# Query projection of a latent attention in 12 tiles instead of 16, with rope parts moved by DMA

## Chip, cores and metric

One core of a Trainium2 chip runs the whole program. The metric is the device time of one execution in microseconds (us), the median of several runs. The engines are TensorE (PE in the profile; its weight loads are PEld), VectorE (DVE), ScalarE (ACT), GpSimd (POOL) and SyncE (SP). SP starts the weight loads; ACT starts a few other transfers from its own queue.

## The reference, cut

Two layers of a decoder trunk on 512 positions of 1024 features, all in float32. The change lies in the latent attention of the first sub-layer: 16 heads, each with 64 features without rope and 32 with rope.

```python
def mla_attention(c_q, c_kv, k_rope, q_norm, w_uq, kv_norm, w_ukv, cos, sin):
    q = (rmsnorm(c_q, q_norm) @ w_uq).reshape(b, s, MLA_HEADS, QK_NOPE + QK_ROPE)
    q_nope = q[..., :QK_NOPE]
    q_pe = apply_rope(q[..., QK_NOPE:], cos[:, :, None, :], sin[:, :, None, :])
    kv = (rmsnorm(c_kv, kv_norm) @ w_ukv).reshape(b, s, MLA_HEADS, QK_NOPE + V_DIM)
    k_nope, v = kv[..., :QK_NOPE], kv[..., QK_NOPE:]
    k_pe = apply_rope(k_rope, cos, sin)          # one for all heads
    ...
        sc = (jnp.einsum('bqhd,bkhd->bhqk', q_nope[:, q0:kend], k_nope[:, :kend])
              + jnp.einsum('bqhr,bkr->bhqk', q_pe[:, q0:kend], k_pe[:, :kend]))
        ...
        pr = jax.nn.softmax(jnp.where(mask, sc, -jnp.inf), axis=-1).astype(v.dtype)
        outs.append(jnp.einsum('bhqk,bkhd->bqhd', pr, v[:, :kend]))
```

`apply_rope` gives t1*cos - t2*sin and t2*cos + t1*sin for the two halves of the 32 features. Around it in each layer stand the input projection, a state-space scan (`ssd`), the output projection, a cross-attention into 256 memory tokens and a gated MLP.

## The kernel before

Activations lie with features on the 128 partitions and the 512 positions along the free axis. Every float32 operand of a large product is split into a high part (float32r, written by ACT) and a low part (the rest, written by DVE or POOL), and `mm3` (L168 to L170) adds three products: high by high, high by low, low by high. Weights are fetched by SP into `wraw` (2 buffers) in the order of a hand-written plan (`specs`), then split by ACT (`whi`, L107) and mostly POOL (`wlo`, L108). All other tiles of 128x512 come from one tag, `unit()`, with `NU` = 68 buffers; PSUM is one tag of 8 banks, `bank()`. The order of TensorE is the order of the program text (`manual_schedule`); the other engines' orders are made by a list scheduler with the program order as priority.

Of the attention: `latent_q` projects the 384 query latents in three tiles and splits them. `front` computes the factors of the norms and the rotated key `kpe`, in generator steps that are interleaved with `inproj`, the projection of the scan's inputs. `prepare`, once, makes the tables `csa` (cos over signed sin, on partitions 64 to 127) and `csb` (the same on partitions 0 to 63), with ones in the other half. `key_tiles` puts the rotated key into the key tiles. `queries(h)` makes one tile of 128 rows for each head: 64 without rope, 32 with rope and the same 32 with their halves swapped. It needs nine matmuls of 128x512 (three `mm3`), one DVE product with the table (L661, it also carries the norm) and a split (L159 ACT, L162 DVE).

In `attention()` each head has one step, and its parts are issued in the order "SKVAMTQ": S scores and softmax of head h, K keys of the next pair (odd h), A product with the values for head h-2, M a tile of the memory keys, T transposes of the probabilities of head h-1, Q the query tile of head h+2. Queries 0 and 1 are made ahead, in `attention_head`. An odd step has K and, from step 3 on, M.

Softmax of one head is four chains: DVE mask and row maximum (L687), ACT exponential (L690), DVE reciprocal (L691), POOL scaling (L692). T is followed by splits (L159, L162) and a copy (L711), A by a copy (L732) and a sum (L733). In `front`, a small product (L455) needs `w`, the end of a chain of small DVE operations (L413 to L428).

## Time and profile before

| what | value |
|---|---|
| median of 3 runs | 1911.72 us (1911.09 to 1911.8) |
| the profiled execution | 1910.9 us |
| its span, first to last instruction | 1909.2 us |
| PE busy | 1871.1 us, 98% |
| DVE, ACT, POOL busy | 1030.6, 950.8, 886.3 us |

The profiled execution is 0.8 us below the median; 1.7 us of it lie outside the span. Busy time counts each engine's compute instructions; a transfer's issue is not in it, though it stands in the timeline on the queue of its engine (ACTq, SPq). Matmul records overlap: their pitch, not their length, is what each costs PE.

### The profile page before, as it was taken

How to read it: one execution, taken by the hardware profiler on the slowest of the kernel's cores; microseconds unless marked ns; L12 is line 12 of the kernel's file. 1: busy time of each engine (PE TensorE's matmuls, PEld its weight loads, DVE VectorE, ACT ScalarE, POOL GpSimd, SP SyncE). 2: the span in 40 equal slices, each digit the busy share in tenths (PEclk: the TensorE clock that was granted, in tenths of full speed). 3: DMA queues.
4: the chain of work that ended last, by engine and by line, in shares of the span. 5: the costliest groups of instructions: out<-in, count | busy, mean ns of one | idle time of the engine just before them, and what ended most of it. 6: DMA issues, size and time to landing. Idle time of an engine off the chain costs nothing.

```text
span 1909.2 us, 24928 instructions
## 1 busy us (share of the span) xinstructions
PE 1871.1 (98%) x9264; PEld 1574.3 (82%) x9264; DVE 1030.6 (54%) x1967; ACT 950.8 (50%) x1694; POOL 886.3 (46%) x563
## 2 busy tenths in 40 slices
PE   8899999999999999999999999999999999999998
PEld 6788889978888888888887887898788888888887
DVE  6777788843343555541137767887334445555312
ACT  5466588843345444433335557887333544444321
POOL 4436455555416444433354454555553354444232
PEclk9999999999999999999999999999999999999999
DMA  5233211332213233232222332113332122222322
GB/s 167 90 119 113 81 55 54 102 111 97 90 33 109 100 100 99 91 101 93 96 95 90 133 108 75 56 61 122 100 100 84 49 100 100 100 95 94 102 91 83
DMA packets 56025, 178.47 MB, mean 93 GB/s; under 512 B 6368, under 2 KB 9312, under 8 KB 55904
## 3 DMA queue, kind: packets, MB, share of 16 engines
q1 hardware_dynamic: 49984, 166.32, 26.4%
q10 hardware_dynamic: 5920, 10.55, 1.8%
q8 instruction: 73, 1.20, 0.3%
q14 instruction: 48, 0.39, 0.1%
HBM read 174.69 MB, written 2.16 MB: 93 GB/s over the span
## 4 chain that ended last, share of the span: by engine, by line
PE 91%; DVE 4%; ACT 2%; POOL 1%; issue 1%; DMA 1%; SPq 0%; ACTq 0%; POOLq 0%; DVEq 0%
PE ps L168 28%; PE ps L170 28%; PE ps L169 28%; PE ps L723 2%; PE ps L704 2%; ACT u L548 1%; POOL wlo L108 1%; DVE u L489 1%; ACT whi L107 1%; PE ps L584 1%; PE ps L578 0%; PE ps L924 0%; PE ps L726 0%; PE ps L558 0%; POOL rstd L271 0%
## 5 line engine op out<-in xcount | busy, mean ns | idle before, releaser
L108 POOL TENSOR_TENSOR wlo<-wraw,whi 128x1024 fp32r<-128x1024 f32 (+1 forms) x290 | 679.9, 2346 | 847.8 <-ACT whi L107 827.8
L168 PE MATMUL ps<-u,whi 128*128 128x512 f32 (+1 forms) x2326 | 899.7, 387 | 9.2 <-ACT whi L107 6.6
L169 PE MATMUL ps<-u,whi 128*128 128x512 f32 (+1 forms) x2326 | 890.6, 383 | 3.8 <-DVE u L165 3.8
L170 PE MATMUL ps<-u,wlo 128*128 128x512 f32 (+1 forms) x2326 | 890.7, 383 | 1.1 <-POOL wlo L108 0.6
L107 ACT ACTIVATE whi<-wraw 128x1024 fp32r<-128x1024 f32 (+2 forms) x319 | 328.2, 1030 | 505.6 <-PE ps L169 402.8
L168 PEld LDWEIGHTS ps<-u,whi 128*128 128x128 f32 x2326 | 439.3, 189 | 93.5 <-ACT whi L107 6.9
L170 PEld LDWEIGHTS ps<-u,wlo 128*128 128x128 f32 x2326 | 439.0, 189 | 87.6 <-POOL wlo L108 1.4
L169 PEld LDWEIGHTS ps<-u,whi 128*128 128x128 f32 x2326 | 439.5, 189 | 86.4 <-DVE u L165 4.9
L162 DVE TENSOR_TENSOR u<-ps,u 128x512 fp32r<-128x512 f32 (+2 forms) x236 | 136.8, 612 | 105.1 <-ACT u L159 104.2
L159 ACT ACTIVATE u<-ps 128x512 fp32r<-128x512 f32 (+2 forms) x236 | 117.3, 540 | 120.7 <-DVE ps L1013 98.3
L1009 DVE SCALAR_TENSOR_TENSOR u<-ps,small,u 128x510 f32<-128x510 f32 (+1 forms) x176 | 131.3, 749 | 74.9 <-ACT u L1007 72.0
L299 POOL TENSOR_TENSOR u<-u,u 128x512 f32<-128x512 f32 (+1 forms) x82 | 102.4, 1249 | 57.7 <-ACT u L298 56.4
L1002 DVE TENSOR_TENSOR ps<-ps,u 128x512 f32<-128x512 f32 x88 | 61.4, 700 | 109.7 <-PE ps L170 101.5
L108 DVE TENSOR_TENSOR wlo<-wraw,whi 128x1024 fp32r<-128x1024 f32 (+1 forms) x29 | 32.5, 1120 | 140.5 <-ACT whi L107 140.4
L692 POOL TENSOR_SCALAR u<-u,rs 128x512 f32<-128x512 f32 (+3 forms) x128 | 66.5, 533 | 78.4 <-DVE rs L691 74.3
L840 DVE TENSOR_TENSOR ps<-ps,u 128x512 f32<-128x512 f32 x32 | 22.4, 700 | 102.7 <-PE ps L170 102.7
L690 ACT ACTIVATE u<-ps,nm 128x512 f32<-128x512 f32 (+3 forms) x128 | 66.2, 524 | 18.0 <-DVE nm L687 12.0
L168 PE MATMUL ps<-u,u 128*128 128x512 f32 (+1 forms) x224 | 73.3, 327 | 0.9 <-ACT u L690 0.9
L489 DVE SCALAR_TENSOR_TENSOR u<-ps,half,u 128x511 f32<-128x511 f32 (+2 forms) x96 | 71.2, 744 | 3.0 <-ACT u L487 1.9
L170 PE MATMUL ps<-u,u 128*128 128x512 f32 (+1 forms) x224 | 72.1, 322 | 0.0
L169 PE MATMUL ps<-u,u 128*128 128x512 f32 (+1 forms) x224 | 72.0, 321 | 0.0
L1007 ACT ACTIVATE u<-ps,small 128x512 f32<-128x512 f32 x88 | 66.8, 761 | 1.7 <-DVE ps L1002 1.5
(193 smaller groups left out, 1765.6 us busy)
## 6 DMA issues: line engine op xcount, KB each, us to landing
wraw<-in_w_up SPq DMA_DIRECT2D x88, 512.0 KB, 3.4
wraw<-in_w_in SPq DMA_DIRECT2D x59, 512.0 KB, 3.5
wraw<-in_w_out SPq DMA_DIRECT2D x32, 512.0 KB, 3.4
wraw<-in_w_down SPq DMA_DIRECT2D x32, 512.0 KB, 3.4
u<-scr ACTq DMA_DIRECT2D x32, 256.0 KB, 4.0
wraw<-in_w_mk SPq DMA_DIRECT2D x16, 512.0 KB, 3.4
wraw<-in_w_mv SPq DMA_DIRECT2D x16, 512.0 KB, 3.5
wraw<-in_w_mq SPq DMA_DIRECT2D x16, 512.0 KB, 3.4
```

The source lines that it names most:

```text
L107: A.activation(hi[:, c], raw[:, c], AF.Copy)
L108: eng.tensor_tensor(lo[:, c], raw[:, c], hi[:, c].bitcast(F32), ALU.subtract)
L159: A.activation(hi, src, AF.Copy)
L162: (leng or V).tensor_tensor(lo, src, hi.bitcast(F32), ALU.subtract)
L168: T.matmul(o, lh, rh, start=start, stop=False)
L169: T.matmul(o, lh, rl, start=False, stop=False)
L170: T.matmul(o, ll, rh, start=False, stop=stop)
L299: (eng or G).tensor_tensor(self.acc, self.acc, sq, ALU.add)
L489: V.scalar_tensor_tensor(r_[:, d:], acc[:, :S - d], cw(3 - d), r_[:, d:], ALU.mult, ALU.add)
L692: G.tensor_scalar(p_[:, :n], p_[:, :n], rs[:, i:i + 1], 1.0, ALU.mult, ALU.mult)
L1007: A.activation(y, acc, AF.Identity, scale=fw(2), bias=par(layer, "ffn_b", ch))
L1009: V.scalar_tensor_tensor(y[:, d:], acc[:, :S - d], fw(2 - d), y[:, d:], ALU.mult, ALU.add)
```

## The change

`queries` now works on 12 tiles in the order `UQ`: a tile of -1 holds the rope parts of four heads (4 x 32 rows), any other the parts without rope of a pair of heads (2 x 64 rows). The swap of the halves and its sign move to the keys: the key tile now holds two rotated forms of the key, one that meets q*cos and one that meets q*sin. `query_rope` makes both products and splits each into one tile of `qph` and `qpl` (one buffer each); `query_pair` then moves, for each head of the pair, 32 rows of each of the four parts beside the head's 64 rows with DMAs that ACT issues. The norm moves from the tables to the latents (`cqr`), and `NU` goes from 68 to 64. The tiles are issued in steps 0, 1, 2, 4, 5, 6, 8, 9, 10 and 12 (`UQ_AT`), two ahead of the loop.

```diff
-NU = 68
+NU = 64
+UQ = (-1, 0, 1, -1, 2, 3, -1, 4, 5, -1, 6, 7)
...
+    UQ_AT = (0, 1, 2, 4, 5, 6, 8, 9, 10, 12)
...
-        for nm, i, n in (("w_uv", 0, 1024), ("w_uk", 0, 1024), ("w_uq", 0, 768)):
+        for nm, i, n in (("w_uv", 0, 1024), ("w_uq", 0, 768), ("w_uk", 0, 1024)):
...
-                elif part == "Q" and h % 2 == 0 and h + 2 < HEADS:
-                    plan("w_uq", layer, h // 2 + 1, 768)
+                elif part == "Q" and h in UQ_AT[::2]:
+                    plan("w_uq", layer, UQ_AT.index(h) // 2 + 1, 768)
...
     def prepare():
-        V.tensor_scalar(rnd, ang, 1.0 / (2 * math.pi), rc[:, 1:2], ALU.mult, ALU.add)
-        V.tensor_scalar(rnd, rnd, magic, None, ALU.add)
+        V.tensor_scalar(rnd, ang, 1.0 / (2 * math.pi), magic, ALU.mult, ALU.add)
...
-        phs = cp.tile([P, 1], F32, name="phs")
-        V.tensor_scalar(phs, rc[:, 1:2], 2 * math.pi, None, ALU.mult)
-        V.tensor_scalar(ang, ang, phs, None, ALU.add)
         V.tensor_scalar(ang, ang, 3.1415925, -3.1415925, ALU.min, ALU.max)
-        A.activation(tab, ang, AF.Sin)
-        V.tensor_scalar(tab, tab, rc[:, 2:3], None, ALU.mult)
-        G.memset(csa[0:64], 1.0)
-        V.tensor_copy(csa[64:128], tab[64:128])
-        V.tensor_copy(csb[0:64], tab[0:64])
-        G.memset(csb[64:128], 1.0)
+        A.activation(css, ang, AF.Sin)
+        A.activation(ang, ang, AF.Abs)
+        A.activation(csc, ang, AF.Sin, scale=-1.0, bias=quart)
...
-        csqa, csqb = unit(), unit()
         def latent_q(i):
             acc = proj(hid, "w_in", layer, i)
-            h_, l_ = unit(F32R), unit(F32R)
-            split(h_, l_, acc, par(layer, "q_norm", i))
+            r_ = unit()
+            A.copy(r_, acc)
             cqs.add(acc)
-            cqh.append(h_)
-            cql.append(l_)
+            cqr.append(r_)
...
         def front():
-            kro, ksh = unit(), unit()
-            V.tensor_tensor(kro[64:128], dtk[64:128], csa[64:128], ALU.mult)
-            A.copy(ksh[64:96], kro[96:128])
-            V.tensor_tensor(kpe[64:96], kro[64:96], ksh[64:96], ALU.add)
-            A.copy(kpe[0:32], kpe[64:96])
+            kro, krs, ksh = unit(), unit(), unit()
+            lo_, hi_ = slice(64, 96), slice(96, 128)
+            V.tensor_tensor(kro[lo_], dtk[lo_], csc[lo_], ALU.mult)
+            V.scalar_tensor_tensor(kro[hi_], dtk[hi_], rc[hi_, 1:2], css[hi_], ALU.mult, ALU.mult)
+            V.tensor_tensor(krs[lo_], dtk[lo_], css[lo_], ALU.mult)
+            V.scalar_tensor_tensor(krs[hi_], dtk[hi_], rc[hi_, 2:3], csc[hi_], ALU.mult, ALU.mult)
+            A.copy(ksh[lo_], kro[hi_])
+            A.copy(ksh[hi_], krs[lo_])
+            V.tensor_tensor(kpe[lo_], kro[lo_], ksh[lo_], ALU.add)
+            V.tensor_tensor(kpe[hi_], krs[hi_], ksh[hi_], ALU.add)
+            A.copy(kpe[0:64], kpe[64:128])
...
             pq = bcast(rq)
-            V.tensor_tensor(csqa, pq, csa, ALU.mult)
-            V.tensor_tensor(csqb, pq, csb, ALU.mult)
+            for i in range(3):
+                V.scalar_tensor_tensor(cqr[i], cqr[i], par(layer, "q_norm", i), pq, ALU.mult, ALU.mult)
+                h_, l_ = unit(F32R), unit(F32R)
+                split(h_, l_, cqr[i])
+                cqh.append(h_)
+                cql.append(l_)
...
         def key_tiles():
-                    for o in (0, 32):
-                        rr = slice(r0 + o, r0 + o + 32)
-                        A.copy(kh_[rr], kpe[r0:r0 + 32])
-                        V.tensor_tensor(kl_[rr], kpe[r0:r0 + 32], kh_[r0:r0 + 32].bitcast(F32), ALU.subtract)
+                    rr = slice(r0, r0 + 64)
+                    A.copy(kh_[rr], kpe[rr])
+                    V.tensor_tensor(kl_[rr], kpe[rr], kh_[rr].bitcast(F32), ALU.subtract)
...
-            V.tensor_tensor(acc, acc, csqb if h % 2 else csqa, ALU.mult)
-            qh, ql = unit(F32R), unit(F32R)
-            split(qh, ql, acc)
-            qq[h] = qh, ql
+        def query_rope(i):
+            acc, sn = query_tile(i), bank()
+            V.tensor_tensor(sn, acc, css, ALU.mult)
+            V.tensor_tensor(acc, acc, csc, ALU.mult)
+            ph, pl = new("qph", (P, 2, S), 1, F32R), new("qpl", (P, 2, S), 1, F32R)
+            for j, src in enumerate((acc, sn)):
+                split(ph[:, j], pl[:, j], src)
+            qpe[0] = ph, pl
+        def query_pair(i, pr):
+            acc = query_tile(i)
+            for j in range(2):
+                qh, ql = unit(F32R), unit(F32R)
+                rows, r0, s0 = slice(64 * j, 64 * j + 64), 64 - 64 * j, 32 * ((2 * pr + j) % 4)
+                for dst, src in zip((qh, ql), qpe[0]):
+                    for c in range(2):
+                        A.dma_start(dst[r0 + 32 * c:r0 + 32 * c + 32].bitcast(F32), src[s0:s0 + 32, c].bitcast(F32))
+                A.activation(qh[rows], acc[rows], AF.Copy)
+                V.tensor_tensor(ql[rows], acc[rows], qh[rows].bitcast(F32), ALU.subtract)
+                qq[2 * pr + j] = qh, ql
...
         def attention_head():
             yield from values(0)
+            query_rope(0)
+            yield
             keys(0)
-            queries(0)
-            yield
-            queries(1)
+            query_pair(1, 0)
             yield
```

`query_tile(i)` is the nine matmuls of `queries`, with a weight load at every even i. `ropec` and `w_uq` are laid out on the host to fit.

## Rows read from the trace of the kernel before

**Rows 1.** Page, part 1: busy us, share of span, instructions.

```profile
PE 1871.1 (98%) x9264; PEld 1574.3 (82%) x9264; DVE 1030.6 (54%) x1967; ACT 950.8 (50%) x1694; POOL 886.3 (46%) x563
```

**Rows 2.** Waits of PE, whole span: total us, times, longest.

```profile
PE ps L168 <- ACT whi L107: 6.6, 1, 6.6
PE ps L455 <- DVE dt L428: 6.5, 2, 4.3
...
PE ps L168 <- ACT u L690: 1.8, 4, 0.5
```

**Rows 3.** Busy time by stretch: PE, PEld, DVE, ACT, POOL, granted clock, DMA share, GB/s.

```profile
217.00:232.00 15.00, 13.13 (x82) 10.30 (x81) 12.53 (x24) 9.45 (x25) 4.23 (x2) 1.00 0.19 62
232.00:356.00 124.00, 122.56 (x765) 110.56 (x764) 101.85 (x302) 103.60 (x258) 73.38 (x80) 1.00 0.18 59
356.00:376.00 20.00, 20.00 (x129) 18.03 (x128) 15.32 (x41) 15.85 (x39) 8.85 (x12) 1.00 0.30 99
...
1173.00:1297.00 124.00, 122.56 (x767) 110.58 (x766) 102.07 (x301) 103.69 (x259) 73.61 (x80) 1.00 0.19 59
```

**Rows 4.** Timeline of PE, one query tile and the scores behind it.

```profile
322.05 0.47 PE L168 MATMUL ps<-u,whi 128*128 128x512 f32 x1
322.37 0.39 PE L169 MATMUL ps<-u,whi 128*128 128x512 f32 x1
...
323.98 0.39 PE L170 MATMUL ps<-u,wlo 128*128 128x512 f32 x1
324.21 0.39 PE L168 MATMUL ps<-u,u 128*128 128x512 f32 x1
```

**Rows 5.** Groups of ACT by shape, 232 to 356 us: busy, mean ns | idle before.

```profile
L159 ACT ACTIVATE u<-ps 128x512 fp32r<-128x512 f32 x27 | 16.1, 598 | 3.3 <-DVE ps L661 3.0
...
L647 ACT ACTIVATE u<-ps 64x512 fp32r<-64x512 f32 x14 | 8.2, 589 | 1.9 <-PE ps L170 1.7
...
L107 ACT ACTIVATE whi<-wraw 128x768 fp32r<-128x768 f32 x6 | 5.1, 842 | 0.1
```

**Rows 6.** Groups of DVE by shape, 232 to 356 us.

```profile
L162 DVE TENSOR_TENSOR u<-ps,u 128x512 fp32r<-128x512 f32 x27 | 18.4, 681 | 1.5 <-ACT u L159 1.3
...
L661 DVE TENSOR_TENSOR ps<-ps,u 128x512 f32<-128x512 f32 x14 | 9.7, 692 | 2.7 <-PE ps L170 2.5
L648 DVE TENSOR_TENSOR u<-ps,u 64x512 fp32r<-64x512 f32 x14 | 9.6, 684 | 1.3 <-ACT u L647 1.2
```

**Rows 7.** Line L501, four transfers of 256 KB that ACT issues for each scan.

```profile
L501 ACTq DMA_DIRECT2D u<-scr x32: 320/451/587, 85.9 to 1147.2; - x32
...
DMA to landing us min/median/max: 3.1/4.0/6.2
```

**Rows 8.** Timeline of ACT, four issues in a row.

```profile
1030.13 0.60 ACT L493 ACTIVATE u<-ps 128x512 f32<-128x512 f32 x1 [0.38 <-DVE ps L480]
1030.13 1.78 ACTq L501 DMA_DIRECT2D u<-scr  x4
1032.04 1.06 ACT L107 ACTIVATE whi<-wraw 128x1024 fp32r<-128x1024 f32 x1 [1.31 <-PE ps L510]
```

**Rows 9.** Timeline of ACT, issues between its operations.

```profile
1079.68 0.34 ACTq L342 DMA_DIRECT2D u<-in_mem  x1
1079.71 0.68 ACT L548 ACTIVATE u<-u,nacs 128x128 f32<-128x128 f32 x2
1080.06 0.45 ACTq L342 DMA_DIRECT2D u<-in_mem  x1
1080.30 0.39 ACT L548 ACTIVATE u<-u,nacs 128x128 f32<-128x128 f32 x1
```

**Rows 10.** Waits of ACT, 232 to 356 us.

```profile
ACT u L690 <- DVE nm L687: 5.3, 10, 1.1
...
ACT f L711 <- DVE u L162: 3.7, 6, 1.0
```

**Rows 11.** Timeline of DVE in the front of layer 0.

```profile
57.59 0.69 DVE L433 TENSOR_TENSOR u<-u,csa 64x512 f32<-64x512 f32 x1
...
59.97 0.68 DVE L435 TENSOR_TENSOR u<-u,u 32x512 f32<-32x512 f32 x1
```

**Rows 12.** Timeline of PE in the front of layer 1.

```profile
1013.17 0.41 PE L455 MATMUL ps<-dt,triu 128*128 128x64 f32 x2 [2.22 <-DVE dt L428]
```

**Rows 13.** Busy time by stretch around the wait of layer 0, columns as in rows 3.

```profile
66.00:70.00 4.00, 0.08 (x1) 0.00 (x0) 4.00 (x6) 0.99 (x2) 2.34 (x1) 0.99 0.08 19
70.00:74.00 4.00, 3.61 (x11) 3.06 (x12) 3.27 (x7) 1.57 (x2) 0.10 (x1) 0.50 0.28 112
74.00:78.00 4.00, 4.00 (x14) 3.17 (x13) 3.93 (x9) 1.50 (x3) 2.28 (x1) 0.66 0.14 30
```

More of the change, by code (lines that the diff above doesn't have):

```diff
@@ L207, in trunk @@
     G.memset(mhalf, -0.5)
+    quart = cp.tile([P, 1], F32, name="quart")
+    G.memset(quart, math.pi / 2)
     half = cp.tile([P, L, 5 * 16 + KD], F32, name="half")
@@ L651, in trunk, with query_tile @@
         qq = {}
-        def queries(h):
-            if h % 2 == 0:
-                uq[0] = weights("w_uq", layer, h // 2)
+        qpe = {}
+        def query_tile(i):
+            if i % 2 == 0:
+                uq[0] = weights("w_uq", layer, i // 2)
             uqh, uql = uq[0]
@@ L784, in attention @@
                         mem_key(MEM_AT.index(h))
-                    elif part == "Q" and h + 2 < HEADS:
-                        queries(h + 2)
+                    elif part == "Q":
+                        queries(h)
                 if h < 2:
```

39 lines of the change are left out of this document (24 added, 15 removed).

## The prediction

> **What bounds the kernel now.** I read the busy shares first. TensorE is busy for 98% of the span, and no other engine is above 54% [rows 1]. Then the waits of TensorE: they are few, and the largest are single events at the start of the program and in the two fronts [rows 2]. So TensorE sets the time almost everywhere, and a matmul taken out of a full stretch should come off the end. An average hides what the stage of the change looks like, so I cut it out: in layer 0, steps 0 to 13 of the attention fill 232 to 356 us, and layer 1 repeats them from 1173 us with the same numbers [rows 3]. There TensorE is full (122.56 of 124 us), but ScalarE and VectorE stand at 84% and 82% (103.60 and 101.85 us). ScalarE has 20.4 us free. That number decides the case, because the change puts its new work there.
>
> **What is removed.** Four query tiles per layer (the ones of steps 3, 7, 11 and 13). The matmul records overlap, so the cost is the distance from the start of a tile to the start of the scores behind it: 324.21 - 322.05 = 2.16 us, 0.24 us for each of nine [rows 4]. Eight tiles are 17.3 us, all on the path as long as TensorE stays the bound: 8.6 us per layer, of which 6.5 lie in 232 to 356 us and 2.16 (step 13) at its end and behind it. Four weight loads with their splits go too (two of them per layer, 0.84 us each on ScalarE [rows 5]). POOL's halves of these splits were ahead of their use, so I count no gain there.
>
> **VectorE in the stage.** Before, 14 tiles cost one product and one subtraction each, 14 x (0.692 + 0.681) = 19.2 us. After, three rope tiles cost two of each, 8.2 us, and seven pairs cost 14 subtractions on 64 rows at 0.684 us (64 rows take as long as 128), 9.6 us [rows 6]. VectorE loses 1.4 us: nothing is gained or lost there.
>
> **ScalarE in the stage.** Before: 14 copies x 0.598 = 8.4 us. After: six for rope, 3.6 us, and 14 on 64 rows at 0.589, 8.2 us [rows 5]. With the two weight splits less this is +1.8 us, 105.4 us in all.
>
> Then the issues: 7 pairs x 2 heads x 4 transfers = 56 per layer in this stage, and eight more ahead of it. No row has a transfer of 32 rows from SBUF to SBUF. The nearest are ScalarE's own issues of 256 KB: 0.32 to 0.59 us each on its queue, median 0.45 [rows 7]. What four of them do to the engine can be seen directly: an operation starts at 1030.13 with the first issue, the four take 1.78 us, and the next operation starts at 1032.04, after 1.31 us of idling [rows 8]. The row names TensorE as the releaser, but the start follows the end of the fourth issue within 0.13 us, so I read the idle time as the issues'. Four cost 1.91 us of the queue, 0.48 each, and 1.31 us of the engine, because one operation ran beside them. The 56 take 26.8 us of the queue. How much of it the engine feels depends on the order:
> - each issue between two operations that are ready: nothing. In rows of layer 1 the issues of the memory tiles stand so, and the operations follow each other without a gap [rows 9].
> - two runs of four for each pair, as the text of `query_pair` has them: 14 x 1.31 = 18.3 us.
> - one run of eight: 8 x 0.48 - 0.60 = 3.2 us, seven times 22.5 us. All eight have their sources ready long before (except behind the first rope tile), while the copy between them waits for the pair's matmuls, so this can happen.
>
> I take 18.3 us and keep 0 and 22.5 as bounds. ScalarE then has 105.4 + 18.3 = 123.7 us. It can't run without gaps: 9.0 us of its waits are for VectorE inside the softmax and behind the transposes [rows 10]. These shrink when ScalarE itself is late, so I keep half, 4.5 us: 128.2 us. TensorE needs 124 - 6.5 = 117.5 us. So ScalarE becomes the bound: the stretch grows by 4.2 us, the rest of the layer still loses 2.16 us, net +2.0 us per layer and +4.1 us for two. What is queued behind the issues on ScalarE are the key copies and the exponentials of the next head; they free the PSUM banks of its scores, and TensorE already waited on just this four times for 1.8 us [rows 2]. The gain goes there.
>
> The Trainium skill (Perfetto Trace Analysis, DMA Instruction — HWDGE) says that the issuing sequencer is free for its next instruction only after the descriptors are generated and the semaphores pushed, and that this is what the profile's record shows. The gap behind the four issues agrees. If by that rule none of the 26.8 us ran beside an operation, the stretch would grow by 12.7 us and the kernel end near 1935. The skill also says (DMA: Bandwidth & Descriptors, Issuing engines are not separate DMA queues) that the time to start a DMA is usually small relative to the DMA itself. Here too the rows agree; but the rule looks at the transfer, and this engine has little time left. By it the issues would count for nothing, as in the first rival.
>
> **Landing.** Transfers of 256 KB land after 3.1 to 6.2 us [rows 7]; these are a quarter of that. A pair made in step h is first read in step h+2, two steps of 8 us or more later, so they are hidden. Only pair 0 is close: its rope tile stands where query 0 stood, about 11 us before the first scores; 2.2 us of matmuls, four operations of 0.7, four issues of 0.48 and at most 6.2 us of landing make 13. I take 0 and keep 2 us per layer as the upper bound.
>
> **Front.** The rotated key needs three products and a sum more on VectorE, 0.69 and 0.68 us each [rows 11], 2.8 us per layer; the scheduler mixes them with the chain that ends in L428, for which TensorE waits at L455: 4.3 us in layer 0 [rows 2], 2.22 us in layer 1 [rows 12]. In layer 0 `prepare` has five VectorE operations less, none longer than these, which about pays for it. The three products and splits of the normed latents come later than the chain, in part. After the 4 us of idling in layer 0 the granted clock is 0.50, then 0.66, the lower of its two levels (1.2 instead of 2.4 GHz) for part of 8 us, which loses 4 x 0.50 + 4 x 0.34 = 3.4 us [rows 13]. So the bounds are wide: if layer 0's wait shrinks enough that the clock stays, -6.8 us; if layer 1's grows by 2.8 us and the clock falls there too, +6.2 us. I take 0 for layer 0 and +2.5 for layer 1.
>
> **The rest.** Loading `w_uq` before `w_uk`, half the key-tile copies, one more sine and an absolute value on ScalarE in a front where it is mostly idle: nothing. The 64 buffers instead of 68 (two less are held by tables, two more by a pair made ahead): no row shows how many are in use. I take nothing; a lack of buffers would show as ScalarE or VectorE waiting for TensorE's last reader, and adds only to the slow side.
>
> **Sum**, against the profiled execution: 1910.9 - 17.3 (tiles) + 21.4 (ScalarE's overrun, 2 x (128.2 - 117.5)) + 2.5 (front) = 1917.5. That execution is 0.8 us below the median of the runs shown, so 1918.3; I say 1918.
>
> **Rivals.**
> 1. *The issues are hidden.* They fall between ready operations as in rows 9, or ScalarE uses its waits for them. It then needs about 105 of 117.5 us, TensorE stays the bound and nearly all of the 17.3 us arrives: 1911.7 - 17.3 + 2.5 + 1 = 1898. For it: 20.4 us are free now. Against it: the eight transfers of a pair become ready together. It decides where the issues cost the engine less than about 13 us per layer. Chance 0.28.
> 2. *A draw.* The issues cost 13 to 17 us per layer; gain and overrun cancel, 1908 to 1915.5. Chance 0.15.
> 3. *Runs of eight, ahead of the next head's exponentials.* 22.5 us, and all 9.0 us of waits remain: 136.9 us, +12.9 - 2.16 per layer, with the front 1936. For it: in an even step TensorE has only scores, values, transposes and a query tile, some 6.5 us, before the next scores need the banks. Against it: a late ScalarE doesn't wait for VectorE as well. Chance 0.12.
>
> The forecast, a small loss (1915.5 to 1930), has 0.45. A change of 0.2%, 3.8 us, is about what a measurement can tell from none: faster 0.28, same 0.15, slower 0.45 + 0.12 = 0.57. The range has to reach into both outer cases: 1897 to 1934.
>
> **What the profile after would show.** PE's count down by 72 matmuls, its busy share in the stage visibly below 98%, with waits for L690 or for splits behind it; ACT's queue with 128 new issues of 0.3 to 0.6 us in runs; key copies and exponentials starting right behind a run. ScalarE idle before them without a named cause would confirm it. I would be wrong if the new issues are shorter than 0.3 us or stand singly between operations, if PE stays full in both stages, or if L455's waits differ by more than 5 us.

## The result, and the profile after

The changed kernel takes 2007.6 us (median of four runs, 2006.9 to 2008.5) against 1911.4 us before, a ratio of 1.051 with a 95% interval of 1.0497 to 1.0523. The prediction had the direction and not the size: 96 us lost instead of 6, and none of its rivals lies near.

Where the time went can be read from landmarks in the two traces: the first softmax maximum of each layer's attention (L687 before, L726 after), the first exponential of the attention to the memory behind it, and the end.

| stretch | before | after | change |
|---|---|---|---|
| start to attention, layer 0 | 233.1 | 246.6 | +13.5 |
| attention to memory attention, layer 0 | 277.0 | 312.1 | +35.1 |
| from there to attention, layer 1 | 663.7 | 674.7 | +10.9 |
| attention to memory attention, layer 1 | 275.3 | 312.2 | +36.8 |
| rest | 460.0 | 460.1 | +0.1 |

The changes are taken before rounding. So 24.4 us are lost in the two fronts, 71.9 us in the two attention stages, and nothing anywhere else.

The busy times of the changed kernel, page part 1 (beside [rows 1]):

```profile
PE 1903.6 (95%) x9192; PEld 1581.1 (79%) x9192; DVE 1054.9 (53%) x1967; ACT 959.7 (48%) x1712; POOL 878.7 (44%) x558
```

There are 72 matmuls fewer, as there should be, and TensorE is nevertheless busy for 32.5 us longer: the same kind of work runs at a lower clock. That shows when the attention of layer 0 is cut out, here for the changed kernel (columns as in [rows 3]):

```profile
core 0: us, PE busy (x) PEld busy (x) DVE busy (x) ACT busy (x) POOL busy (x), PEclk, DMA share, GB/s
246.60:433.60 187.00, 163.06 (x884) 136.22 (x883) 128.71 (x347) 126.77 (x306) 81.58 (x90) 0.91 0.24 72
```

The kernel before, from the same landmark to the last head's sum:

```profile
233.10:383.70 150.60, 149.16 (x924) 134.11 (x923) 123.36 (x347) 123.81 (x300) 84.99 (x92) 1.00 0.21 70
```

TensorE idled for 1.4 us of 150.6 there. Now it idles for 23.9 us and its mean granted clock is 0.91. Neither VectorE (128.71) nor ScalarE (126.77) is full. The waits of TensorE over the whole span of the changed kernel (beside [rows 2]):

```profile
PE ps L465 <- DVE dt L426: 13.6, 2, 8.9
PE ps L743 <- DVE u L694: 10.8, 8, 4.1
...
PE ps L743 <- ACT u L729: 5.4, 6, 1.7
```

L465 is the front's wait for the time steps (L455 before), 13.6 us instead of 6.5. The others are new: transposes (L743) that wait for a subtraction of the query pair (L694) and for exponentials (L729). The longest, 4.1 us, comes once in each layer; of the others in layer 0's attention none is above 1.6 us. Some of them cost more than their length, by the clock. Four stretches of 4 us in that stage:

```profile
284.00:288.00 4.00, 2.94 (x26) 2.70 (x25) 1.90 (x4) 1.72 (x4) 0.06 (x1) 1.00 0.33 79
288.00:292.00 4.00, 3.12 (x15) 2.34 (x14) 3.43 (x7) 3.60 (x10) 3.47 (x4) 0.75 0.00 2
292.00:296.00 4.00, 2.97 (x9) 1.75 (x8) 3.88 (x10) 2.62 (x7) 1.88 (x3) 0.50 0.34 131
296.00:300.00 4.00, 3.65 (x15) 3.55 (x16) 2.58 (x12) 2.88 (x11) 2.06 (x4) 0.50 0.01 2
```

Two waits (1.06 us before 287.7 and 0.89 before 289.9) come ahead of the fall: the granted clock is 1.00 from 289 to 290 us and 0.50 from 290 to 291, the lower of the two levels (1.2 instead of 2.4 GHz). Two more (0.76 and 0.62 us) follow at the lower level. A score matmul of 128x256 takes 0.41 us at 293.8 and 0.28 us at 303.9, where the clock is back.

What starts such waits is seen on ScalarE's own timeline. ACTq is its queue; "x2" are two issues in a row:

```profile
302.52 1.16 ACTq L692 DMA_DIRECT2D u<-qph  x2
303.21 0.36 ACT L163 ACTIVATE u<-ps 128x256 fp32r<-128x256 f32 x1
303.47 0.26 ACT L750 COPY f<-ps 128x128 f32<-128x128 f32 x1
304.05 1.16 ACTq L692 DMA_DIRECT2D u<-qpl  x2
305.26 0.59 ACT L693 ACTIVATE u<-ps 64x512 fp32r<-64x512 f32 x1 [1.53 <-POOL wlo L112]
305.28 1.21 ACTq L692 DMA_DIRECT2D u<-qph  x2
306.53 1.25 ACTq L692 DMA_DIRECT2D u<-qpl  x2
307.83 0.59 ACT L693 ACTIVATE u<-ps 64x512 fp32r<-64x512 f32 x1 [1.98 <-issue]
308.44 0.69 ACT L729 ACTIVATE u<-ps,nm 128x512 f32<-128x512 f32 x1
```

and on VectorE's, same kernel and time:

```profile
303.98 0.14 DVE L726 DVE_READ_ACCUMULATOR2_ANT nm<- 128x1 f32 x1
...
305.95 0.68 DVE L694 TENSOR_TENSOR u<-ps,u 64x512 fp32r<-64x512 f32 x1 [0.64 <-ACT u L693]
```

The maximum that the first exponential needs is there at 304.12. The exponential starts at 308.44: six issues and two copies were ahead of it. This is the run of issues that the prediction described, and its cost to the engine is somewhat above what it said (1.53 and 1.98 us of idling for four issues, against 1.31). The landing is harmless (median us in the last column):

```profile
u<-qph ACTq DMA_DIRECT2D x64, 64.0 KB, 2.0
u<-qpl ACTq DMA_DIRECT2D x64, 64.0 KB, 2.0
```

ScalarE's waits in that stage do name landings of moves:

```profile
ACT u L693 <- DMA u<-qph: 10.2, 5, 2.4
```

But 30 of the 32 copies L693 start 0.05 us behind the end of the last issue ahead of them (307.78 and 307.83 above), while two to five moves have yet to land. So these waits are time of the issues.

In the fronts VectorE has no gap while TensorE waits, and the clock falls behind the wait in both layers, where before it fell only in layer 0 ([rows 13]):

```profile
72.00:81.00 9.00, 0.47 (x3) 0.07 (x1) 9.00 (x20) 2.53 (x5) 2.34 (x1) 0.50 0.16 58
81.00:85.00 4.00, 3.62 (x11) 3.08 (x12) 4.00 (x9) 1.81 (x4) 0.00 (x0) 0.50 0.00 0
...
1067.00:1071.00 4.00, 3.71 (x11) 3.16 (x12) 3.96 (x6) 2.04 (x3) 2.37 (x1) 0.50 0.00 0
```

### The profile page after: what moved, and what is told of

It is laid out like the page before. It is cut to its first block, busy times and chain, and to the rows that moved or that the text cites. A ratio compares the mean times of both kernels' runs of the same rounds, so it can differ in the third digit from the quotient of the medians.

```text
span 2005.6 us, 25014 instructions
## 1 busy us (share of the span) xinstructions
PE 1903.6 (95%) x9192; PEld 1581.1 (79%) x9192; DVE 1054.9 (53%) x1967; ACT 959.7 (48%) x1712; POOL 878.7 (44%) x558
## 4 chain that ended last, share of the span: by engine, by line
PE 79%; DVE 8%; ACT 5%; DMA 3%; issue 2%; POOL 1%; ACTq 1%; SPq 0%; POOLq 0%; DVEq 0%
PE ps L172 25%; PE ps L173 25%; PE ps L174 24%; PE ps L762 1%; POOL wlo L112 1%; PE ps L743 1%; ACTq L692 1%; ACT u L729 1%; DVE u L499 1%; DMA wraw<-in_w_mv 1%; DMA u<-qph 1%; DVE ps L726 1%; ACT whi L111 1%; DVE u L166 1%; DVE u L169 1%
## 5 line engine op out<-in xcount | busy, mean ns | idle before, releaser
L111 ACT ACTIVATE whi<-wraw 128x1024 fp32r<-128x1024 f32 (+2 forms) x315 | 325.1, 1033 | 536.7 <-PE ps L173 440.3
L166 DVE TENSOR_TENSOR u<-ps,u 128x512 fp32r<-128x512 f32 (+2 forms) x204 | 116.8, 602 | 96.2 <-ACT u L163 95.3
L163 ACT ACTIVATE u<-ps 128x512 fp32r<-128x512 f32 (+2 forms) x204 | 100.5, 530 | 114.6 <-DVE ps L1052 98.4
L112 DVE TENSOR_TENSOR wlo<-wraw,whi 128x1024 fp32r<-128x1024 f32 (+1 forms) x29 | 32.4, 1119 | 139.5 <-ACT whi L111 139.5
L172 PE MATMUL ps<-u,u 128*128 128x512 f32 (+1 forms) x224 | 79.0, 353 | 19.1 <-ACT u L656 4.2
L173 PE MATMUL ps<-u,u 128*128 128x512 f32 (+1 forms) x224 | 75.3, 336 | 1.2 <-DVE u L657 1.1
L729 ACT ACTIVATE u<-ps,nm 128x512 f32<-128x512 f32 (+3 forms) x128 | 66.5, 528 | 19.3 <-DVE nm L726 16.3
L174 PE MATMUL ps<-u,u 128*128 128x512 f32 (+1 forms) x224 | 74.4, 332 | 0.0
L726 DVE CUSTOM_DVE_ANT_0 ps<-ps,mask 128x512 f32<-128x512 f32 (+3 forms) x128 | 61.5, 500 | 21.9 <-PE ps L174 21.2
```

The lines of the kernel that those rows point to most:

```text
L111: A.activation(hi[:, c], raw[:, c], AF.Copy)
L112: eng.tensor_tensor(lo[:, c], raw[:, c], hi[:, c].bitcast(F32), ALU.subtract)
L163: A.activation(hi, src, AF.Copy)
L166: (leng or V).tensor_tensor(lo, src, hi.bitcast(F32), ALU.subtract)
L172: T.matmul(o, lh, rh, start=start, stop=False)
L173: T.matmul(o, lh, rl, start=False, stop=False)
```

## Experiments

Five theories were on the table. A: the issues' time on ScalarE's queue. B: moves and weight loads wait for each other's landing. C: too few buffers. D: copies wait for the landing of moves into the same tile. F: the front's added VectorE work. G, H and T came up on the way. Times are medians; the kernel before ran at 1909.6 to 1910.9 beside them. Edits are against the changed kernel unless the name begins with "before".

**1. late_front.** The rotated key and the normed latents behind the chain of the time steps.

```diff
         def front():
-            kro, krs, ksh = unit(), unit(), unit()
...
-            A.copy(kpe[0:64], kpe[64:128])
             rq = rstd_cols(cqs.acc, QL, rx)
             yield
             rk = rstd_cols(cks.acc, KVL, rx)
             yield
-            pq = bcast(rq)
...
-            yield
             pk = bcast(rk)
...
             A.dma_start(scr, acsT)
             yield
+            kro, krs, ksh = unit(), unit(), unit()
...
+            yield
+            pq = bcast(rq)
...
```

> The changed kernel with the key's rotation and the normed query latents moved behind the chain that ends in the time steps, so that VectorE does that chain first, as before the change. Theory F (the fronts lose 23 us because the added VectorE products stand ahead of the chain TensorE waits for, and the granted clock falls after the longer wait): 1985 to 1993 us, TensorE's wait for the time steps back to 4 to 7 us over both layers. Rival (the added work has to be done before the first scores anyway, so the loss only moves behind the chain): 2003 to 2010 us, with as much waiting at the scan's end instead. The attention stages should stay as in the changed kernel by either, 186 us each.

2015.6 us. The chain ended at 70.3 us as before the change (81.2 in the changed kernel), but one `yield` less had brought the sums of the time steps forward in TensorE's order by one projection, so that the longest wait for them was still 9.1 us. The run told nothing on F; it was made again as run 9.

**2. before_dummy_moves.** Beside this edit, `NU = 66` makes room for the tiles `dump`.

```diff
             split(qh, ql, acc)
             qq[h] = qh, ql
+            for k in range(4):
+                A.dma_start(dump[32 * k:32 * k + 32], kpe[64:96])
```

> The kernel before, plus four transfers of 32 rows per head from ScalarE into a tile that nobody reads: 128 issues, no one waits for what they bring. Theory A or B (the issues' own time on ScalarE's queue, or their completion semaphores shared with the weight loads): 1950 to 1985 us, TensorE's idle time in the attention up by some 15 to 25 us a layer and the granted clock below 0.95 there. Theory C or D (fewer buffers, or the copies into the same tile waiting for the transfers to land): at most 1926 us, since no buffer and no reader is touched.

1922.9 us, and this was no test of A. ScalarE's order puts a transfer where its source is ready, and this source is ready in the front. The first and the last issue ahead of the attention of layer 0 in this kernel:

```profile
87.18 0.71 ACTq L667 DMA_DIRECT2D dump<-u  x1
...
199.68 0.51 ACTq L667 DMA_DIRECT2D dump<-u  x1
```

No issue stands in the attention itself (it takes 150.6 us, unchanged); all the loss is in the fronts and scans.

**3. before_64_buffers.** `NU = 68` to `NU = 64` in the kernel before.

> The kernel before with 64 instead of 68 shared buffers and nothing else. Theory C (the loss is a lack of buffers): 1930 us or more. Theories A, B and D: 1908 to 1916 us.

1913.4 us, ratio 1.0013 (1.0001 to 1.0024). The kernel before hardly misses four buffers. I took this to end theory C, too early, as runs 15, 17 and 18 show.

**4. moves_from_gpsimd**, and **7. moves_from_sync** (the same with `nc.sync.dma_start`).

```diff
-                        A.dma_start(dst[r0 + 32 * c:r0 + 32 * c + 32].bitcast(F32), src[s0:s0 + 32, c].bitcast(F32))
+                        G.dma_start(dst[r0 + 32 * c:r0 + 32 * c + 32].bitcast(F32), src[s0:s0 + 32, c].bitcast(F32))
```

> The changed kernel with the 128 moves issued from GpSimd's queue instead of ScalarE's; sources, targets, landing and buffers as they were. Theory A (issue time on ScalarE's queue): most of the attention's 73 us comes back, 1930 to 1955 us, with the granted clock of the attention stages above 0.97. Theory D (the copies wait for the landing of the moves into the same tile) or C (buffers): 2000 us or more, since these waits stay. Theory B (shared completion semaphores): between, and the weight loads on SyncE's queue still wait for moves.

> The changed kernel with the 128 moves issued from SyncE's queue, which also holds the weight loads; ScalarE issues none of them. Theories A and G (both place the loss on ScalarE's queue): 1915 to 1945 us. Theory B (moves and weight loads wait for each other through shared completion semaphores): 1990 us or more, as both stand on one queue now. A rival of its own: a move waits behind a load whose buffer is not free yet, and the scores wait for the move; then 1945 to 1990 us with TensorE waiting for moves by name.

1976.0 and 1967.5 us. So 40 of the 96 us belong to ScalarE's queue, and B is out as the main cause: of the three queues the one that holds the weight loads too is the fastest. But 57 us stay with ScalarE free of all issues, outside what A allowed. The attention of layer 0 on SyncE's queue:

```profile
245.20:413.70 168.50, 151.23 (x891) 131.79 (x891) 126.85 (x345) 126.35 (x304) 80.24 (x89) 0.97 0.27 79
```

and what SyncE's queue waited for there (L692 are the moves):

```profile
SPq L692 <- PE ps L174: 11.7, 6, 7.0
SPq L692 <- PE ps L743: 9.7, 4, 5.2
...
SPq L692 <- PE ps L762: 2.1, 2, 1.5
```

The sources are long ready; the moves wait for TensorE, which is still reading the buffers that they are to write. That pointed back to the buffers.

**5. copies_first**, **6. copies_first_split.** Both copies and subtractions of a pair ahead of its eight moves (shown); in the second, the second head's four moves stand behind the next step's scores.

```diff
-                for dst, src in zip((qh, ql), qpe[0]):
-                    for c in range(2):
...
                 qq[2 * pr + j] = qh, ql
+            for k in range(2):
+                for j in range(2):
+                    r0, s0 = 64 - 64 * j, 32 * ((2 * pr + j) % 4)
+                    dst, src = qq[2 * pr + j][k], qpe[0][k]
+                    for c in range(2):
...
```

> The changed kernel with one reordering: of each pair, both copies and both subtractions stand first, and the eight moves behind them in one run. Theory G (the loss is order: the copy that frees the pair's PSUM bank stands behind four issues, VectorE's subtraction behind that copy, and VectorE's softmax work and TensorE's next bank behind that subtraction): 1930 to 1965 us, and TensorE's waits for the subtraction L694 gone. Theory A (the issues' time itself): 1995 to 2015 us, since as many issues stand on the same queue.

> As the run before, and the four moves of a pair's second head are issued one step later, behind that step's scores, so that runs are of four, not of eight. Theory G: within 8 us of the run before, since nothing that frees a bank stands behind them in either. If it is the length of a run that delays the exponentials (theory A in its form of runs): 10 to 25 us below the run before.

2003.7 and 2001.6 us. Theory G is out as the main cause: TensorE's waits for the subtraction went, others (for key copies and exponentials) came in their place. D is out with it: nothing is behind the moves there that writes the same tile, and the copies of the changed kernel start before the moves land.

**8. before_dummy_ahead.** The dummies of run 2 ahead of the query's split, again with `NU = 66`.

```diff
             V.tensor_tensor(acc, acc, csqb if h % 2 else csqa, ALU.mult)
+            for k in range(4):
+                A.dma_start(dump[32 * k:32 * k + 32], kpe[64:96])
             qh, ql = unit(F32R), unit(F32R)
             split(qh, ql, acc)
```

> The kernel before with the same four dummy transfers per head as in the earlier run, but issued between a query's product on VectorE and its copy on ScalarE, so that the copy that frees the PSUM bank stands behind them. Theory G: 1940 us or more, against 1922.9 with the dummies behind the copy. Theory A: 1918 to 1928 us, no difference by place.

1923.4 us, and no test either: the issues stand in the scan again, for the same reason, and the attention takes 150.8 us.

**9. late_front_2.** As run 1, with the missing `yield` put back and the latents six projections later.

```diff
             rk = rstd_cols(cks.acc, KVL, rx)
             yield
+            yield
             pk = bcast(rk)
...
+            for i in range(6):
+                yield
             pq = bcast(rq)
```

> The changed kernel with the key's rotation moved behind the chain of the time steps and the normed query latents six projections later, and this time with the sums of the time steps at the place in TensorE's order that they have in the kernel before (in the first try they came one projection, 5.8 us, earlier, so that the wait stayed at 9.1 us). Theory F: 1985 to 1995 us, TensorE's wait for the time steps at most 7 us over both layers. Rival: the added work delays the scan wherever it stands; 2003 us or more.

2003.7 us, 4 less than the changed kernel. TensorE's waits in this kernel:

```profile
PE ps L597 <- ACT u L580: 12.0, 4, 6.3
...
PE ps L447 <- DVE dt L426: 4.1, 2, 2.5
```

The wait for the time steps is down from 13.6 to 4.1 us; four waits of 12.0 us together in the scan have taken its place. At this later place the work isn't hidden either.

**10. before_short_tiles.** One matmul instead of nine in the four query tiles that the change drops.

```diff
+                if h in (5, 9, 13, 15):
+                    if k == 0:
+                        T.matmul(acc, uqh[:, o:o + P], cqh[k], start=True, stop=True)
+                else:
+                    mm3(acc, uqh[:, o:o + P], uql[:, o:o + P], cqh[k], cql[k], k == 0, k == 2)
```

> The kernel before, in which the four query tiles per layer that the change removes (those of steps 3, 7, 11 and 13) keep their product, copy and subtraction but have one matmul instead of nine, so the queries of four heads per layer are not computed in full. Nothing is moved and nothing is added. My prediction's first term (a matmul taken out of a full stretch comes off the end): 8 x 1.92 = 15.4 us less, 1895 us. Theory H (these tiles cover the time between a head's transposes and the values that need them split, so TensorE waits where they stood and the granted clock falls behind the wait): 1903 us or more, up to no gain at all.

1905.4 us, ratio 0.9975 (0.9964 to 0.9986): 5.5 us gained, where 15.4 were taken away. Its attention of layer 0:

```profile
233.30:381.20 147.90, 143.53 (x888) 127.41 (x888) 124.09 (x347) 123.14 (x300) 84.11 (x91) 1.00 0.22 70
```

TensorE's busy time fell by 5.6 us and its idle time rose from 1.4 to 4.4 us. What it waits for there, above all (L694 is the exponential in this kernel, L727 the product with the values):

```profile
PE ps L168 <- ACT u L694: 1.7, 3, 0.8
PE ps L727 <- ACT u L159: 1.1, 3, 0.5
```

**11. no_moves.** Copy and subtraction of each head on all 128 rows of the pair's tile, no transfer.

```diff
-                for dst, src in zip((qh, ql), qpe[0]):
...
-                A.activation(qh[rows], acc[rows], AF.Copy)
-                V.tensor_tensor(ql[rows], acc[rows], qh[rows].bitcast(F32), ALU.subtract)
+                A.activation(qh, acc, AF.Copy)
+                V.tensor_tensor(ql, acc, qh.bitcast(F32), ALU.subtract)
```

> The changed kernel without the 128 moves: the copy and the subtraction of each head take all 128 rows of the pair's tile, so the rope part of the queries is left out, and only the rope tiles' own work stays. Theory A (all the attention's loss is the moves): 1905 to 1925 us, that is the front's loss and the tiles' gain. Theory H (the missing tiles are the other part): about 1955 to 1970 us, as with the moves on SyncE's queue, which would show that the moves cost nothing there.

1943.1 us. Without any move the change still costs 32 us, so with the rest of it as it stands no way of moving the rope parts could make it pay. It lies between the two expectations.

**12. sync_late_memory.** Run 7 with the memory key's tile behind the transposes in the steps 3, 7, 11 and 13.

```diff
-                for part in (FIRST if h == 0 else ORDER if h + 2 < HEADS else LAST):
+                for part in ("SKVATM" if h in (3, 7, 11, 13) else FIRST if h == 0 else ORDER if h + 2 < HEADS else LAST):
```

> The moves on SyncE's queue, and in the steps 3, 7, 11 and 13, which have no query tile, the memory key's tile is computed behind the transposes instead of ahead of them, so that it covers their splits. Theory H: TensorE's waits for the split at the values (16.4 us in six waits) mostly gone, 1940 to 1955 us against 1967.5. Rival (the order inside a step does not matter, ScalarE and VectorE are late anyway): 1962 to 1972 us.

1967.0 us, no change. In layer 0 the waits of the values (L762) for their splits fell from 8.2 to 1.2 us, as H says, and waits of the transposes (L743) for key subtractions (3.2 us) and of scores for exponentials came in their place. The place of the wait is H's; filling it gains nothing.

**13. half_moves**, **14. dump_moves**, **15. after_60_buffers**: moves of 64 rows (run 13, shown); no_moves with the 128 issues into tiles that nobody reads and 60 buffers (run 14); the changed kernel with 60 buffers (run 15).

```diff
-                    for c in range(2):
-                        A.dma_start(dst[r0 + 32 * c:r0 + 32 * c + 32].bitcast(F32), src[s0:s0 + 32, c].bitcast(F32))
+                    A.dma_start(dst[r0:r0 + 64].bitcast(F32), src[s0 // 64 * 64:s0 // 64 * 64 + 64, j].bitcast(F32))
```

```diff
+                for dst, src in zip(dump[pr % 2], qpe[0]):
+                    for c in range(2):
+                        A.dma_start(dst[r0 + 32 * c:r0 + 32 * c + 32].bitcast(F32), src[s0:s0 + 32, c].bitcast(F32))
```

The second diff is run 14's, against no_moves.

> The changed kernel with 64 moves of 64 rows instead of 128 of 32: half the issues, the same bytes, the same targets and readers. The rows that are moved are not the right ones, so the rope part of the queries is wrong. Theory A (the number of issues on ScalarE's queue): about half of the 40 us that SyncE's queue gave back, 1980 to 1992 us. Theory T (the moves' ties: target buffers, landing, readers): 2002 to 2010 us, since these are the same.

> The kernel without moves, plus the 128 issues from ScalarE with the sources of the change, into four tiles that nobody reads; 60 shared buffers to make room. The rope part of the queries is left out. Theory A in full (issues are all of the moves' 64 us): 1998 to 2012 us. Theory A for 40 of them and theory T for 24: 1975 to 1992 us. Theory T for all: 1943 to 1955 us.

> The changed kernel with 60 shared buffers instead of 64, for comparison with the run before this one too. Theory C in its remaining form (the moves' targets are held longer and buffers run short): 2020 us or more. Otherwise 2005 to 2012 us, as the kernel before lost 2.6 us with four less.

1984.3, 1986.3 and 2021.4 us. Half the issues give back 23 us. Issues into tiles that nobody reads leave 35.1 us less than the real moves (runs 14 and 15, both with 60 buffers). That isn't the targets and readers alone, since the issues stand elsewhere too: in layer 0's attention 23.3 us of run 15's have no operation beside them, and 2.7 us of run 14's. And four buffers less cost the changed kernel 13.8 us, five times what they cost the kernel before: theory C was not dead. In run 14 most issues stand singly between operations, as its ScalarE timeline shows:

```profile
310.07 0.69 ACT L730 ACTIVATE u<-ps,nm 128x512 f32<-128x512 f32 x1
310.12 0.51 ACTq L693 DMA_DIRECT2D dump<-qph  x1
```

**16. no_moves_old_front**: no_moves with the front's work of before, the new table code kept. **17. no_moves_60** and **18. no_moves_68**: no_moves with 60 and with 68 buffers.

```diff
-            r_ = unit()
-            A.copy(r_, acc)
+            h_, l_ = unit(F32R), unit(F32R)
+            split(h_, l_, acc, par(layer, "q_norm", i))
...
+            V.tensor_tensor(kro[64:128], dtk[64:128], csc[64:128], ALU.mult)
+            A.copy(ksh[64:96], kro[96:128])
+            V.tensor_tensor(kpe[64:96], kro[64:96], ksh[64:96], ALU.add)
...
+            V.tensor_tensor(csqa, pq, csc, ALU.mult)
+            V.tensor_tensor(csqb, pq, css, ALU.mult)
```

Run 18, beside its `NU = 68`:

```diff
-            ph, pl = new("qph", (P, 2, S), 1, F32R), new("qpl", (P, 2, S), 1, F32R)
-            for j, src in enumerate((acc, sn)):
-                split(ph[:, j], pl[:, j], src)
-            qpe[0] = ph, pl
+            for src in (acc, sn):
+                split(unit(F32R), unit(F32R), src)
```

> The kernel without moves, with the front's work of the kernel before: the query latents split at once and not normed there, one product and one sum for the rotated key, and two products for the tables; the new table code stays. Values are left out or differ, the tiles' own work stays. Theory F (added work in the front): 20 us off 1943.1, 1920 to 1926 us, both fronts back within 3 us of before. Rival (the tables' three functions now stand ahead of the exponential of the time steps in layer 0): layer 0 keeps most of its 13 us, 1930 to 1936 us.

> The kernel without moves with 60 shared buffers; the rope part of the queries is left out. If the buffers are short only because the moves hold their targets: within 4 us of the 1943.1 with 64, and then the issues by themselves cost 43 us. If they are short without moves too, as the 14 us of the changed kernel suggest: 1950 to 1960 us, and the issues cost 26 to 36.

> The kernel without moves with 68 shared buffers: the rope tiles are split into four of them, which are free again at once, instead of into two tables of their own. The rope part of the queries is left out. If the attention's remaining 8 us a layer are a lack of buffers: 1927 to 1935 us, attention 148 to 151 us. If they are the order of the tiles and their waits: 1939 to 1945 us, attention 153 to 157 us.

1936.2 us: the fronts are back within 3.5 us (layer 0) and 4.3 us (layer 1) of before, so some 15 of the 23 us that no_moves loses there are the added work. The length of TensorE's wait doesn't tell that. In this run it is as long in layer 0 as in no_moves (9.3 us), but it ends at 72.6 instead of 82.1 us:

```profile
72.56 0.66 PE L461 MATMUL ps<-dt,triu 128*128 128x64 f32 x2 [9.35 <-DVE dt L428]
```

The total missed its band because the attention, which the edit doesn't touch, became 4 us and 3 us longer. Then 1954.1 us with 60 buffers and 1934.5 with 68, against 1943.1 with 64. The attention of layer 0 with 68, 64 and 60 buffers, one fence for each of these three kernels:

```profile
244.00:395.80 151.80, 143.65 (x887) 126.98 (x886) 123.69 (x346) 125.93 (x306) 81.80 (x90) 1.00 0.19 64
```

```profile
246.10:401.40 155.30, 145.81 (x887) 128.51 (x886) 124.37 (x345) 124.84 (x304) 81.50 (x90) 0.99 0.19 63
```

```profile
245.40:407.70 162.30, 150.41 (x884) 131.62 (x883) 123.81 (x345) 125.99 (x304) 81.25 (x90) 0.96 0.18 59
```

Same matmuls, same operations: the idle time of TensorE is 8.2, 9.5 and 11.9 us, and the clock goes from 1.00 to 0.96. Run 18 differs from run 11 by the place of the rope tiles' splits as well, and its two executions lie 6 us apart (1931.4 and 1937.6), so the 9 us between them are rough.

Run 14 has 128 issues more than run 17 and costs 1986.26 - 1954.12 = 32.1 us more. In layer 0's attention its TensorE idles for 18.0 us, against 11.9, and two waits make up nearly all of the difference. From the timelines of run 14 (ScalarE, TensorE, VectorE):

```profile
254.35 0.84 ACT L111 ACTIVATE whi<-wraw 128x768 fp32r<-128x768 f32 x1 [1.77 <-PE ps L174]
255.10 1.69 ACT L168 ACTIVATE u<-u,small 128x256 fp32r<-128x256 f32 x4
258.82 1.54 PE L744 MATMUL ps<-ident,u 128*128 128x128 f32 x6 [4.12 <-DVE u L600]
282.69 2.31 DVE L269 TENSOR_SCALAR tiny<-tiny 128x4 f32<-128x4 f32 x1
287.97 1.52 PE L763 MATMUL ps<-u,u 128*128 128x512 f32 x2 [3.80 <-ACT u L163]
```

and the same places in run 17:

```profile
253.28 1.69 ACT L168 ACTIVATE u<-u,small 128x256 fp32r<-128x256 f32 x4
255.99 0.84 ACT L111 ACTIVATE whi<-wraw 128x768 fp32r<-128x768 f32 x1
256.73 1.21 PE L739 MATMUL ps<-ident,u 128*128 128x128 f32 x6 [0.88 <-DVE u L599]
281.80 0.61 DVE L269 TENSOR_SCALAR tiny<-tiny 128x4 f32<-128x4 f32 x1
283.54 0.90 PE L758 MATMUL ps<-u,u 128*128 128x512 f32 x3 [1.25 <-DVE u L166]
```

In neither wait does an issue hold up what TensorE needs. In the first, the list scheduler has put a weight split (L111), which waits for TensorE's last read of its buffer, ahead of the splits of the memory tokens (L168) on ScalarE, and VectorE's half of these splits stands ahead of the operation that TensorE waits for (L600). Run 17 has the two the other way round. In the second, a small VectorE operation is late (last section), and ScalarE idles for 3.67 us until 286.40 with no issue on its queue.

**The sum of it**, from the kernel before to the changed one. The lines add up because "left over" is what remains:

| step | us | from |
|---|---|---|
| tiles shortened | -5.5 | run 10 against before |
| fronts | +19.3 | landmarks of no_moves_68 (24.4 in the changed kernel) |
| left over (rope tiles, order of the tiles) | +10 | 1934.5 - 1910.9 + 5.5 - 19.3 |
| four buffers fewer | +9 | 1943.1 - 1934.5 |
| the moves, from SyncE | +24 | 1967.5 - 1943.1 |
| the moves on ScalarE instead | +40 | 2007.6 - 1967.5 |

Each edit also gives the list scheduler another order of ScalarE and VectorE. No run holds that order fixed, so every line contains what the order does.

And what it is made of in the attention of layer 0 (TensorE busy and clock from the view of busy time between the same landmarks; idle is the difference):

| kernel | stretch | TensorE busy | idle | clock |
|---|---|---|---|---|
| before | 150.6 | 149.2 | 1.4 | 1.00 |
| before_short_tiles | 147.9 | 143.5 | 4.4 | 1.00 |
| no_moves_68 | 151.8 | 143.7 | 8.2 | 1.00 |
| no_moves | 155.3 | 145.8 | 9.5 | 0.99 |
| moves_from_sync | 168.5 | 151.2 | 17.3 | 0.97 |
| half_moves | 175.0 | 156.5 | 18.5 | 0.94 |
| after | 187.0 | 163.1 | 23.9 | 0.91 |

From short tiles to after, TensorE idles 19.5 us more and is busy 19.5 us longer for the same work; 0.09 of 187.0 us, some 17 us, is the lower clock. That isn't a fixed price: in no_moves_68 TensorE idles 3.8 us more than with short tiles, its clock stays at 1.00, and it is busy for as long.

## Why the prediction was wrong, step by step

**The tiles, -17.3 us.** "A matmul taken out of a full stretch should come off the end." Run 10: 5.5 us came off for 15.4 removed. A busy share of 98% says that TensorE rarely waits, not that the next wait is far. In each layer 7.7 us of matmuls went. In the attention of layer 0, 2.9 us of it came back as idling: scores that wait for exponentials to free their banks (1.7 us in three waits) and values that wait for the splits of the transposes (1.6 us in five, three of them for ScalarE). TensorE's busy time fell by 5.6 us only; the other 2 us aren't explained. The moves make the waits of the values longer, 8.2 us in run 7, but run 12 took those away and gained nothing.

**VectorE, nothing.** Held as far as work goes: 123.4 us in the attention of layer 0 before, 123.7 in no_moves_68. The 128.7 us of the changed kernel are the same operations: their lengths add up to 1.9 us more (147.4 against 145.5), 1.6 of it one L269 (last section), and the rest is that fewer of the records overlap.

**ScalarE's issues, 18.3 us per layer in the stage.** Nearly right as a size. Most issues take 0.51 to 0.61 us, not 0.48; the 56 in the attention of layer 0 take 32.4 us of the queue, and for 22.9 us of it no operation runs beside them (both added up from the records of L692). The rule of the Trainium skill that was quoted (Perfetto Trace Analysis, DMA Instruction — HWDGE: the sequencer is held until the descriptors are made) agrees with these rows. The Trainium skill's other rule (DMA: Bandwidth & Descriptors, Issuing engines are not separate DMA queues: the start is usually small beside the DMA) does not help here: 0.51 to 0.61 us of issue stand against 2.0 us to landing.

**The overrun, 2 x (128.2 - 117.5).** This step failed. It gave +2.0 us per layer with the tiles' gain in it; the attention grew by 35.1 and 36.8 us. It treated the stage as a race of full engines: the one with most work sets the time. After the change ScalarE is busy for 126.8 us and held by issues for 22.9 of 187.0, together 80%, no fuller than before (123.8 of 150.6, 82%), and every other engine has time left too. What the runs put in its place: 40 us of the loss belong to the issues on ScalarE's queue (run 7), 24 us to the moves even when SyncE issues them (runs 7 and 11), and 9 us to four buffers.

Why short delays cost so much is argued, not shown by a run of its own: scores, maximum, exponential, scaling, transposes, split and values of neighbouring heads form a loop through four engines with few PSUM banks and buffers between them. What is late at one place in it makes the next engine wait, and the free time of the delayed engine lies elsewhere in the loop. The cost doesn't start at "about 13 us per layer" either: with half the issues 6.5 us in layer 0's attention have no operation beside them, instead of 22.9, and 17 of the 40 us remain (runs 13 and 7).

**The clock** was priced only in the front. In the attention of layer 0 it fell four times: during the wait of 4.1 us that ends at 261.4, and behind several waits of 0.6 to 1.2 us near 290, 341 and 379 us. It makes up some 17 of the 39 us between short tiles and the changed kernel.

**The runs of issues.** "Each issue between two operations that are ready: nothing." Run 14 has mostly that, with 2.7 us of 28.3 uncovered in layer 0's attention, and costs 32.1 us all the same. The traces show where its extra idling is: two waits of 4.12 and 3.80 us in each layer, against 0.88 and 1.25 us in layer 0 of run 17, from another order on ScalarE and a late operation on VectorE. The lower clock behind them (0.94 against 0.96) goes with 6.0 us more of busy time. The wait of 4.1 to 4.2 us at this place is in the changed kernel and in runs 5, 6, 13 and 14, all with issues on ScalarE, and not in runs 11 and 17 (0.9 us). So part of what counts as the issues' cost is the order that the scheduler makes around them; how much a fixed order would save was not tested.

**Landing, 0.** Right: 2.0 us. What was missing is the other end of a transfer. A move needs its target free, and waits for it at the head of an in-order queue. Run 7 shows the wait by name, and against run 11 the moves cost 24 us there without an issue on ScalarE; the 35 us between runs 14 and 15 contain the other places of the issues too. Which of the two it is was not separated.

**The front, +2.5 us.** It was 24.4. The working had VectorE's added 2.8 us pay against five operations saved in layer 0. But VectorE is without a gap there (9.00 of 9.00 us), and its order puts one other operation between nearly every two of the chain, so what is added delays its end; it came 11 us later. Run 16 returns 15 us by taking the added work out; run 9's later place gained 4 us.

**Buffers, 0.** "No row shows how many are in use. I take nothing." Four are worth 9 us (runs 11 and 18), 11 us (runs 11 and 17) or 14 us (run 15 and the change) here, and 2.6 us in the kernel before. That the kernel before doesn't need them says little of a kernel whose transfers hold them longer.

Of what should show it, the signs that were named came (new issues of 0.5 to 0.6 us in runs, exponentials right behind them, ScalarE idle without a named cause). None of them carried the size. One sign of being wrong came as well: the waits at L465 are 7.1 us longer than those at L455 (13.6 against 6.5).

## What to carry to other kernels

In a loop through several engines with few buffers, don't sum the work per engine and take the largest: look for what each edit puts between two links of the loop, count the buffers that it holds, and where the clock of the full engine falls behind short waits, add what the lower level costs (here some 17 us beside 19.5 us of idling). Before counting on a removed matmul, shorten it alone in the old kernel; here that one run would have shown that a third of the gain exists. A transfer on a compute engine's queue costs its issue time and waits in line for its target's last reader; a dummy copy of it tests that only if its source becomes ready at the same moment. And where a scheduler orders the engines, compare the orders of two runs before a difference is put down to the edit.

## What had not been expected of the hardware

A small operation on VectorE took as long as GpSimd's operation beside it. On SyncE's run, VectorE first, then GpSimd:

```profile
283.42 1.88 DVE L269 TENSOR_SCALAR tiny<-tiny 128x4 f32<-128x4 f32 x1
285.33 0.69 DVE L772 TENSOR_TENSOR u<-ps,u 64x512 f32<-64x512 f32 x1
```

```profile
282.90 2.37 POOL L112 TENSOR_TENSOR wlo<-wraw,whi 128x1024 fp32r<-128x1024 f32 x1
```

Four elements per row took 1.88 us and ended at 285.30, with the weight split on GpSimd (285.27). The head's sum (L772) behind it was late, then the square and the splits on ScalarE, then the values: this is how the wait of 3.35 us at 287.6 came about. In the changed kernel the same line (ns: lowest, median, highest):

```profile
L269 DVE TENSOR_SCALAR tiny<-tiny x17: 160/1824/2243, 37.1 to 1997.7; 128x4 f32<-128x4 f32 x14, 128x2 f32<-128x2 f32 x3
```

Six of the 17 have no GpSimd operation beside them and take 0.16 to 0.17 us; of the eleven others ten take 1.23 to 2.24 us. The Trainium skill (SBUF — State Buffer, SBUF: two separate sides) describes it: a pair of ports is shared by VectorE and GpSimd as an exclusive lock for a whole instruction, and the other engine blocks. The rows agree. What was not expected is that the smallest operations of a chain are hit as hard as the large ones, and that one of them stands behind some of TensorE's longest waits, 3.35 us in run 7 and 3.80 us in run 14. It isn't what the loss hangs on: in runs 5 and 6 this L269 takes 0.15 and 0.20 us, and they are only 4 and 6 us faster than the changed kernel.
